# First stage of a hybrid decoder layer: the first two products' loads in written order, the later loads held back, a result tile moved to its own slots

## The chip, the cores and the metric

The kernel runs on one core of a Trainium2 chip. The metric is the device time of one execution in microseconds (us); the median of several runs counts. Engines are named as in the profile: PE does matmuls, PEld loads their weights, DVE, ACT and POOL do elementwise work, and SP issues nearly all DMAs from one in-order queue (SPq).

## What is computed

```
h = x @ w_in                  # x 1024 x 2048; w_in 2048 x 5392, float32
q_a, k_a, v_a, z_a, q_g, k_g, v_g, z_g, gk_lr = split(h)
y_a = sliding_window_attention(rope(q_a), rope(k_a), v_a, sinks) * silu(z_a)
y_g = rmsnorm(gated_linear_attention(q_g, k_g, v_g, decay(gk_lr))) * silu(z_g)
x = layer_norm(alpha * x + concat(y_a, y_g) @ w_out)
```

The first stage of the kernel, the only one that the change touches, computes `v_g = x @ w_v` with x 1024 x 2048 and w_v 2048 x 1024.

## The kernel before

The product for `v_g` is cut into 2 x 2 blocks and made by seven block products instead of eight (Strassen's scheme in Winograd's form). They run in the order 1, 2, 7, 5, 6, 4, 3 (`v_seq`). Each block product is 512 x 1024 by 1024 x 512 and has eight steps k = 0 to 7. A step takes one tile of x (128 x 512, 256 KB) and half of a weight tile (128 x 1024, 512 KB, two steps). Each float32 operand is split into a high part (a cast on ACT, L98) and a low part (a subtraction on DVE, L99), and a step is 4 row blocks times 3 matmuls: high by high (L696), high by low (L697), low by high (L698). So a step is 12 matmuls and a product 96.

Products 1 and 2 take x and w as they are in memory. Product 2 adds into product 1's banks, after `v_collect` has copied these out to the `u` tiles. Product 7 takes differences of two loaded tiles, made on POOL (L619 for x, L644 for w). Products 5, 6, 4 and 3 take running sums in tiles of their own, `xsum0` to `xsum7` and `wsum0` to `wsum3`: product 5 loads them first, and later products add or subtract one more loaded tile on POOL (L626 for x, L650 for w). Product 3's w is loaded as it is.

The pools set what can be loaded early: four slots for raw weights (tag `raw`), eight for split weights, 16 slots `xh` and 16 slots `xl` that loaded and split x tiles share. A load into a slot waits until the slot's last reader is done, and all that stands behind it in the SP queue waits with it.

Who stands where in an engine's queue is decided by the Tile scheduler, which goes by its own estimate of time and by `high_priority`. `fetch` (L600 to L605) issues every load of this stage at raised priority. `load_consts` (L122) loads the small tables and the tile `w_up`; it is called after product 1. `begin` (L551) loads `w_gk` for the second stage. `v_collect` for product 6 makes the result `o` (L668, L669) in a `raw` slot and writes it to memory from there (L670). `order(ins, head)` adds a scheduling dependency without a semaphore, so that the scheduler places `ins` behind `head`.

After this stage `begin(0)` loads x again for the second stage, with a few small matmuls (`lracc`, L283) between those of product 3.

Of the kernel before, what the change touches and what calls it, by code (L numbers as in the profile page):

```python
# [7 lines left out]
F32 = mybir.dt.float32  # L8
# [8 lines left out]
P = 128  # L17
# [55 lines left out]
def build(ctx: ExitStack, tc, xT, xr, w_e, w_v, w_gk, w_up, b_gk, cos_d, sin_d, cst_d, sinks, wn_d, w_out, g_d, b_d, out):  # L73
# [45 lines left out]
    one = cp.tile([P, 1], F32, name="one")  # L119
    mhalf = cp.tile([P, 2], F32, name="mhalf")  # L120

    def load_consts():  # L122
        wup = raw_p.tile([P, 2, 512], F32, name="raw", tag="raw")[:, 0]
        for t, src in ((cst, cst_d), (wup, w_up), (bgk, b_gk), (sink, sinks), (wn, wn_d)):
            SP.dma_start(t, src)
        V.tensor_scalar(nsink, sink, -1.0, None, ALU.mult)
        V.tensor_scalar(wnh, wn, 0.5, None, ALU.mult)
        A.copy(wuph, wup)
        V.tensor_tensor(wupl, wup, wuph.bitcast(F32), ALU.subtract)
        G.memset(neg, NEG)  # L130
        G.memset(one, 1.0)
        G.memset(mhalf, -0.5)
# [283 lines left out]
    def order(ins, head):  # L416
        with_dep = mybir.DependencyInfo(mybir.DependencyClass.NoSync, mybir.DependencyReason.DATA)
        tc.add_manual_dep(ins.ins, head.ins.name, with_dep, reason="after the bank's first")
        return ins
# [130 lines left out]
    def begin(H, i):  # L550

        c = ctxs[H]
        new_lr(H)
        parts[i], parts[i + 1] = [], []
        xr = []
        with tc.high_priority(2000):
            c["wgk"] = cp.tile([P, KT * 32], F32, name="wgk", tag="lr")
            SP.dma_start(c["wgk"], w_gk)
        for q in range(4):
            for j in range(2):  # L560
                xr += load(xT[H, q][:, 1024 * j:1024 * j + 1024])
                if j == 0 and q % 2 == 0:
                    wr = [load(jobs[i + n].src[0][:, 512 * q:512 * q + 1024]) for n in range(2)]
            for n in range(2):
                parts[i + n].append(split(wr[n][q % 2], w_p, "w"))
            for k in range(4 * q, 4 * q + 4):
                with tc.high_priority():
                    low_rank(c["lracc"], c["wgk"], k, xr[k])
                c["x"].append(split(xr[k], x_p, "x"))
        load_tabs(H)  # L570
# [26 lines left out]
    wsum = [vp.tile([P, 2, 512], F32, name=f"wsum{k}") for k in range(4)]  # L597
    us = {(i, t): vp.tile([P, 512], F32, name=f"u{i}{t}") for i in (1, 5, 7) for t in range(NB)}

    def fetch(t, src, pieces=1):  # L600
        with tc.high_priority(2000):
            for u in range(pieces):
                o = t[:, u:u + 1] if pieces > 1 else t
                SP.dma_start(o, src[:, 512 * u:512 * u + 512].unsqueeze(1) if pieces > 1 else src)
        return t  # L605

    def v_x(i, k):

        def block(h, g):
            return xT[h, 2 * g + k // 4][:, (k % 4) * T:(k % 4 + 1) * T]  # L610

        def raw(h, g, tag):
            return fetch(x_p.tile([P, T], F32, name="yr", tag=tag), block(h, g))

        if i in (1, 2, 4):
            a = raw(*{1: (0, 0), 2: (0, 1), 4: (1, 1)}[i], "xh")
        elif i == 7:
            a = raw(0, 0, "xh")
            G.tensor_tensor(a, a, raw(1, 0, "xl"), ALU.subtract)  # L619
        else:  # L620

            a = xsum[k]
            if i == 5:
                fetch(a, block(1, 0))
            b = raw(*{5: (1, 1), 6: (0, 0), 3: (0, 1)}[i], "xl")
            G.tensor_tensor(a, a, b, ALU.add if i == 3 else ALU.subtract)  # L626
        return split(a, x_p, "x")

    def v_w(i, kp):

        def block(g, F):
            return w_v[F, 2 * g + kp // 2][:, (kp % 2) * 1024:(kp % 2) * 1024 + 1024]

        def raw(g, F):
            r = raw_p.tile([P, 2, 512], F32, name="raw", tag="raw")
            if i == 1 and kp == 0:
                return fetch(r, block(g, F), 2)
            return fetch(r, block(g, F).rearrange("p (u c) -> p u c", u=2))

        if i in (1, 2, 3):  # L640
            r = raw(*{1: (0, 0), 2: (1, 0), 3: (1, 1)}[i])
        elif i == 7:
            r = raw(0, 1)
            G.tensor_tensor(r, r, raw(1, 1), ALU.add)  # L644
        else:

            r = wsum[kp]
            if i == 5:
                fetch(r, block(0, 0).rearrange("p (u c) -> p u c", u=2))
            G.tensor_tensor(r, r, raw(*{5: (0, 1), 6: (1, 1), 4: (1, 0)}[i]), ALU.add)  # L650
        return [split(r[:, u], w_p, "w") for u in range(2)]

    def v_collect(i, t, acc):
        u1, u5, u7 = (us[j, t] for j in (1, 5, 7))
        if i == 1:
            A.copy(u1, acc)
        elif i == 2:
            o = us[5, t]
            A.copy(o, acc)
            SP.dma_start(vd[0][0][:, t], o)  # L660
        elif i == 7:
            A.copy(u7, acc)
        elif i == 5:
            A.copy(u5, acc)
        elif i == 6:
            V.tensor_tensor(u1, u1, acc, ALU.add)
            V.tensor_tensor(u7, u7, u1, ALU.add)
            o = raw_p.tile([P, 512], F32, name="raw", tag="raw")  # L668
            V.tensor_tensor(o, u5, u7, ALU.subtract)  # L669
            SP.dma_start(vd[1][1][:, t], o)  # L670
            V.tensor_tensor(u5, u5, u1, ALU.subtract)
        else:
            o = u7 if i == 4 else u5
            V.tensor_tensor(o, o, acc, ALU.add)
            SP.dma_start(vd[1 if i == 4 else 0][0 if i == 4 else 1][:, t], o)

    v_seq = (1, 2, 7, 5, 6, 4, 3)
    v_xs, v_acc, v_n = {}, None, 0
    for vn, i in enumerate(v_seq):
        if i != 2:  # L680
            v_acc = []
            for t in range(NB):
                pool, tag = (mm, "mm") if v_n % 8 < 3 else (vo, "vo")
                v_acc.append(pool.tile([P, 512], F32, name="accv", tag=tag))
                v_n += 1
        for k in range(8):
            if (i, k) not in v_xs:
                v_xs[i, k] = v_x(i, k)
            if k % 2 == 0:
                wv = v_w(i, k // 2)  # L690
            if vn + 1 < len(v_seq):
                v_xs[v_seq[vn + 1], k] = v_x(v_seq[vn + 1], k)
            (xh, xl), (wh, wl) = v_xs[i, k], wv[k % 2]
            for t in range(NB):
                c = slice(t * P, t * P + P)
                PE.matmul(v_acc[t], xh[:, c], wh, start=(k == 0 and i != 2), stop=False, skip_group_check=True)  # L696
                PE.matmul(v_acc[t], xh[:, c], wl, start=False, stop=False, skip_group_check=True)  # L697
                PE.matmul(v_acc[t], xl[:, c], wh, start=False, stop=(k == 7 and i != 1), skip_group_check=True)  # L698
        for t in range(NB):
            v_collect(i, t, v_acc[t])  # L700
        if i == 1:
            load_consts()
    v_st.close()
    ap = side.enter_context(tc.tile_pool(name="ap", bufs=1, reuse_waits="tile"))
    gp = side.enter_context(tc.tile_pool(name="gp", bufs=1, reuse_waits="tile"))
# [11 lines left out]
    i = 0  # L717
# [248 lines left out]
```

## Time and profile before

| | |
|---|---|
| median of three runs | 1526.32 us (1522.78 to 1526.6) |
| the profiled execution's own time | 1524.23 us |
| its span | 1522.3 us |
| PE busy | 1416.3 us (93% of the span) |
| DVE / ACT / POOL busy | 941.6 / 624.6 / 384.3 us |
| mean granted TensorE clock | 0.971 of full speed |

A span is the time from the first to the last recorded instruction; 1.9 us of the execution lie outside of it. Busy shares are averages over stages with different limits, so the first stage has to be read from its own stretch, which is the first 253 us.

### The profile page before, as it was taken

To read this page: it belongs to the slowest core of one execution; us is meant where nothing else is said; L and a number is where in the kernel's file an instruction comes from. 1 tells how busy PE (TensorE), PEld (TensorE's weight loads), DVE (VectorE), ACT (ScalarE), POOL (GpSimd) and SP (SyncE) were. 2 spreads that over 40 slices of the span, in tenths; PEclk is the share of its full clock that TensorE was granted. 3 is DMA by queue.
4 is the path that set the end of the run, shared out by engine and by line. 5 is a ranking of instruction groups with operands and counts; after the bars stand their busy time and mean duration, and the time that the engine had idled before them with its cause. 6 is when DMAs were issued, how large, how long until landed. Compare 5 with 4: busy or idle time off the path is not lost.

```text
span 1522.3 us, 22157 instructions
## 1 busy us (share of the span) xinstructions
PE 1416.3 (93%) x8128; PEld 1133.0 (74%) x8128; DVE 941.6 (62%) x1545; ACT 624.6 (41%) x1335; POOL 384.3 (25%) x373
## 2 busy tenths in 40 slices
PE   3877679999999999999999999999999799999996
PEld 2664556888878877876888888887887588888885
DVE  3445476486666666568676657557658444455798
ACT  3322234454354354355454455344345324333320
POOL 0267041222323124122223222123221412023000
PEclk7899979999999999999999999999999899999998
DMA  9482167543443444445444443353345597766452
GB/s 333 152 268 93 35 224 239 166 148 122 153 141 122 136 144 133 135 152 170 156 157 149 142 144 120 121 163 113 116 160 159 154 344 242 241 187 217 138 213 111
DMA packets 116413, 251.66 MB, mean 165 GB/s; under 512 B 12368, under 2 KB 49232, under 8 KB 115152
## 3 DMA queue, kind: packets, MB, share of 16 engines
q1 hardware_dynamic: 115152, 248.15, 50.1%
q10 hardware_dynamic: 1152, 2.10, 0.4%
q8 instruction: 64, 1.05, 0.3%
q14 instruction: 45, 0.37, 0.1%
HBM read 205.63 MB, written 39.85 MB: 161 GB/s over the span
## 4 chain that ended last, share of the span: by engine, by line
PE 77%; DVE 6%; DMA 3%; ACT 2%; issue 2%; POOL 1%; SPq 0%; DVEq 0%; ACTq 0%; POOLq 0%
PE acc L159 15%; PE acc L161 14%; PE acc L160 14%; PE acco L798 6%; PE acco L796 6%; PE acco L797 6%; PE po L264 2%; PE accv L696 2%; PE accv L698 2%; PE accv L697 2%; DVE wl L99 1%; PE ps L232 1%; PE ps L233 1%; DMA yr<-yd 1%; DVE dd L316 1%
## 5 line engine op out<-in xcount | busy, mean ns | idle before, releaser
L99 DVE TENSOR_TENSOR wl<-raw,wh 128x512 fp32r<-128x512 f32 x408 | 317.8, 788 | 180.1 <-ACT wh L98 174.1
L159 PE MATMUL acc<-xh,wh 128*128 128x512 f32 x1088 | 428.7, 394 | 0.0
L160 PE MATMUL acc<-xl,wh 128*128 128x512 f32 x1088 | 428.0, 393 | 0.0
L161 PE MATMUL acc<-xh,wl 128*128 128x512 f32 x1088 | 427.3, 393 | 0.0
L98 ACT CAST wh<-raw 128x512 fp32r<-128x512 f32 x408 | 246.6, 618 | 270.3 <-PE acc L160 195.8
L161 PEld LDWEIGHTS acc<-xh,wl 128*128 128x128 f32 x1088 | 204.8, 188 | 47.3 <-issue 6.1
L159 PEld LDWEIGHTS acc<-xh,wh 128*128 128x128 f32 x1088 | 204.6, 188 | 45.5 <-issue 3.4
L160 PEld LDWEIGHTS acc<-xl,wh 128*128 128x128 f32 x1088 | 204.6, 188 | 41.9 <-issue 1.8
L797 PE MATMUL acco<-wl,xh 128*128 128x512 f32 x416 | 162.8, 391 | 0.0
L796 PE MATMUL acco<-wh,xh 128*128 128x512 f32 x416 | 162.5, 392 | 0.0
L798 PE MATMUL acco<-wh,xl 128*128 128x512 f32 x416 | 162.4, 391 | 0.0
L696 PE MATMUL accv<-wh,xh 128*128 128x512 f32 x224 | 94.6, 430 | 70.3 <-ACT xh L98 46.2
L99 DVE TENSOR_TENSOR xl<-yr,xh 128x512 fp32r<-128x512 f32 x88 | 68.4, 781 | 132.9 <-ACT xh L98 131.9
L98 ACT CAST xh<-yr 128x512 fp32r<-128x512 f32 x88 | 54.0, 620 | 212.5 <-POOL yr L775 71.5
L696 PEld LDWEIGHTS accv<-wh,xh 128*128 128x128 f32 x224 | 45.3, 203 | 89.0 <-ACT xh L98 54.3
L697 PE MATMUL accv<-wl,xh 128*128 128x512 f32 x224 | 94.2, 421 | 0.5 <-DVE wl L99 0.4
L797 PEld LDWEIGHTS acco<-wl,xh 128*128 128x128 f32 x416 | 78.7, 189 | 17.0 <-DVE wl L99 0.5
L796 PEld LDWEIGHTS acco<-wh,xh 128*128 128x128 f32 x416 | 78.7, 189 | 16.3
L798 PEld LDWEIGHTS acco<-wh,xl 128*128 128x128 f32 x416 | 78.5, 189 | 16.4
L580 POOL TENSOR_TENSOR raw<-raw 128x256 f32<-128x256 f32 x32 | 26.1, 814 | 224.5 <-DMA raw<-in_w_out_dram 163.5
L698 PE MATMUL accv<-wh,xl 128*128 128x512 f32 x224 | 80.2, 416 | 1.6 <-DVE xl L99 1.5
L775 POOL TENSOR_TENSOR yr<-yr 128x512 f32<-128x512 f32 x32 | 44.2, 1383 | 145.7 <-DMA yr<-yd 107.7
(186 smaller groups left out, 1918.5 us busy)
## 6 DMA issues: line engine op xcount, KB each, us to landing
raw<-in_w_e_dram SPq DMA_DIRECT2D x136, 512.0 KB, 4.3
yr<-yd SPq DMA_DIRECT2D x88, 256.0 KB, 4.6
yr<-in_xT_dram SPq DMA_DIRECT2D x64, 256.0 KB, 5.3
raw<-in_w_out_dram SPq DMA_DIRECT2D x128, 128.0 KB, 2.7
td<-raw SPq DMA_DIRECT2D x32, 512.0 KB, 3.4
raw<-td SPq DMA_DIRECT2D x32, 512.0 KB, 5.3
raw<-in_w_v_dram SPq DMA_DIRECT2D x31, 512.0 KB, 5.1
raw<-in_w_out_dram SPq DMA_DIRECT2D x24, 512.0 KB, 3.9
```

The source lines that it names most:

```text
L98: A.copy(hi, src)
L99: V.tensor_tensor(lo, src, hi.bitcast(F32), ALU.subtract)
L159: PE.matmul(acc, wh[:, c], xh, start=(k == 0), stop=False)
L160: PE.matmul(acc, wh[:, c], xl, start=False, stop=False)
L161: PE.matmul(acc, wl[:, c], xh, start=False, stop=(k == KT - 1))
L696: PE.matmul(v_acc[t], xh[:, c], wh, start=(k == 0 and i != 2), stop=False, skip_group_check=True)
L697: PE.matmul(v_acc[t], xh[:, c], wl, start=False, stop=False, skip_group_check=True)
L698: PE.matmul(v_acc[t], xl[:, c], wh, start=False, stop=(k == 7 and i != 1), skip_group_check=True)
L775: G.tensor_tensor(a, a, b, ALU.add if sign > 0 else ALU.subtract)
L796: PE.matmul(acc, yh[:, c], wh, start=(first and k == 0), stop=False, skip_group_check=True)
L797: PE.matmul(acc, yh[:, c], wl, start=False, stop=False, skip_group_check=True)
L798: PE.matmul(acc, yl[:, c], wh, start=False, stop=(last and k == 7), skip_group_check=True)
```

## The change

- The loads of products 1 and 2 are issued at ordinary priority and kept in the order of the program. Product 2's x tiles are written two at a time into product 1's steps 4 to 7, instead of one per step.
- The first loads of the running sums are placed behind named matmuls: `xsum`k behind the last matmul of product 2's step k, `wsum`kp behind that of product 7's step 2 kp.
- The constants and `w_gk` are placed behind product 6's last matmul, and `load_consts` is called after product 6.
- Product 6's result `o` gets two slots of its own instead of `raw` slots.

```diff
-    def load_consts():
+    def load_consts(head):
         wup = raw_p.tile([P, 2, 512], F32, name="raw", tag="raw")[:, 0]
         for t, src in ((cst, cst_d), (wup, w_up), (bgk, b_gk), (sink, sinks), (wn, wn_d)):
-            SP.dma_start(t, src)
+            order(SP.dma_start(t, src), head)
...
             c["wgk"] = cp.tile([P, KT * 32], F32, name="wgk", tag="lr")
-            SP.dma_start(c["wgk"], w_gk)
+            ins = SP.dma_start(c["wgk"], w_gk)
+            if H == 0:
+                order(ins, v_last[6, 7])
...
-    def fetch(t, src, pieces=1):
-        with tc.high_priority(2000):
+    v_last = {}
+
+    def fetch(t, src, pieces=1, head=None):
+        with tc.high_priority(2000 if head or len(v_last) > 8 else 0):
             for u in range(pieces):
                 o = t[:, u:u + 1] if pieces > 1 else t
-                SP.dma_start(o, src[:, 512 * u:512 * u + 512].unsqueeze(1) if pieces > 1 else src)
+                ins = SP.dma_start(o, src[:, 512 * u:512 * u + 512].unsqueeze(1) if pieces > 1 else src)
+                if head:
+                    order(ins, head)
+                elif len(v_last) <= 8:
+                    tc.keep_in_program_order(ins)
         return t
...
             if i == 5:
-                fetch(a, block(1, 0))
+                fetch(a, block(1, 0), head=v_last[2, k])
...
             if i == 5:
-                fetch(r, block(0, 0).rearrange("p (u c) -> p u c", u=2))
+                fetch(r, block(0, 0).rearrange("p (u c) -> p u c", u=2), head=v_last[7, 2 * kp])
...
-            o = raw_p.tile([P, 512], F32, name="raw", tag="raw")
+            o = vp.tile([P, 512], F32, name="o", tag="o", bufs=2)
             V.tensor_tensor(o, u5, u7, ALU.subtract)
...
             if vn + 1 < len(v_seq):
-                v_xs[v_seq[vn + 1], k] = v_x(v_seq[vn + 1], k)
+                for k2 in ((k,) if vn else (2 * k - 8, 2 * k - 7)):
+                    if k2 >= 0:
+                        v_xs[v_seq[vn + 1], k2] = v_x(v_seq[vn + 1], k2)
...
-                PE.matmul(v_acc[t], xl[:, c], wh, start=False, stop=(k == 7 and i != 1), skip_group_check=True)
+                v_last[i, k] = PE.matmul(v_acc[t], xl[:, c], wh, start=False, stop=(k == 7 and i != 1), skip_group_check=True)
         for t in range(NB):
             v_collect(i, t, v_acc[t])
-        if i == 1:
-            load_consts()
+        if i == 6:
+            load_consts(v_last[6, 7])
```

Three places of the built queues are shown. In all of them `yr` is a loaded x tile, `raw` a loaded weight tile, and the number behind a name tells tiles apart.

The SP queue, start of the program, before: behind the first loads of product 1 stand all eight `xsum` loads (and then the four of `wsum`).

```order
L604 DMA raw_212<-in_w_v_dram 128x1024
L604 DMA yr_164<-in_xT_dram 128x512
L604 DMA raw_270<-in_w_v_dram 128x1024
L604 DMA raw_328<-in_w_v_dram 128x1024
L604 DMA xsum0_119<-in_xT_dram 128x512
L604 DMA xsum1_120<-in_xT_dram 128x512
L604 DMA xsum2_121<-in_xT_dram 128x512
L604 DMA xsum3_122<-in_xT_dram 128x512
L604 DMA xsum4_123<-in_xT_dram 128x512
L604 DMA yr_182<-in_xT_dram 128x512
L604 DMA xsum5_124<-in_xT_dram 128x512
```

The same place with the change; `yr_147`, `yr_176`, `yr_194`, `yr_222`, `yr_240`, `yr_280`, `yr_310` and `yr_350` are product 1's x tiles, the other `yr` up to `yr_362` product 2's.

```order
L608 DMA yr_176<-in_xT_dram 128x512
L608 DMA yr_194<-in_xT_dram 128x512
L608 DMA raw_200<-in_w_v_dram 128x1024
L608 DMA yr_222<-in_xT_dram 128x512
L608 DMA yr_240<-in_xT_dram 128x512
L608 DMA raw_246<-in_w_v_dram 128x1024
L608 DMA yr_256<-in_xT_dram 128x512
L608 DMA yr_262<-in_xT_dram 128x512
L608 DMA yr_280<-in_xT_dram 128x512
L608 DMA yr_286<-in_xT_dram 128x512
L608 DMA yr_292<-in_xT_dram 128x512
L608 DMA yr_310<-in_xT_dram 128x512
```

The sums' loads have left the head of the queue (the first, `xsum0`, stands at place 27 now), and the x tiles of product 2 stand between those of product 1.

The SP queue where product 2's result is written out (`vd0_0` from `u50` and so on), before; `yr_511` and `yr_513` are the pair of product 7's step 4.

```order
L604 DMA raw_888<-in_w_v_dram 128x1024
L604 DMA yr_511<-in_xT_dram 128x512
L604 DMA yr_513<-in_xT_dram 128x512
L604 DMA raw_938<-in_w_v_dram 128x1024
L604 DMA raw_988<-in_w_v_dram 128x1024
L660 DMA vd0_0_101<-u50_135 128x512
L660 DMA vd0_0_101<-u51_136 128x512
```

The same with the change; `yr_467` and `yr_469` are the pair of product 7's step 3.

```order
L608 DMA wsum0_127<-in_w_v_dram 128x1024
L668 DMA vd0_0_101<-u50_135 128x512
L608 DMA raw_825<-in_w_v_dram 128x1024
L668 DMA vd0_0_101<-u51_136 128x512
L668 DMA vd0_0_101<-u52_137 128x512
L608 DMA raw_875<-in_w_v_dram 128x1024
L608 DMA yr_467<-in_xT_dram 128x512
L668 DMA vd0_0_101<-u53_138 128x512
L608 DMA yr_469<-in_xT_dram 128x512
```

Before, five of product 7's eight pairs stand ahead of the write; now three do, and the fourth stands behind it.

The SP queue at the end of product 6, before; `raw_1261` to `raw_1408` are product 4's weights, `vd1_1` the write of product 6's result.

```order
L670 DMA vd1_1_104<-raw_1235 128x512
L670 DMA vd1_1_104<-raw_1241 128x512
L604 DMA yr_1197<-in_xT_dram 128x512
L670 DMA vd1_1_104<-raw_1247 128x512
L604 DMA raw_1261<-in_w_v_dram 128x1024
L604 DMA raw_1310<-in_w_v_dram 128x1024
```

With the change:

```order
L125 DMA cst_72<-in_cst_dram 128x705
L125 DMA raw_1244<-in_w_up_dram 128x512
L608 DMA raw_1261<-in_w_v_dram 128x1024
L608 DMA raw_1310<-in_w_v_dram 128x1024
L608 DMA yr_1090<-in_xT_dram 128x512
L608 DMA raw_1359<-in_w_v_dram 128x1024
L125 DMA bgk_75<-in_b_gk_dram 128x4
L125 DMA sink_76<-in_sinks_dram 128x16
L125 DMA wn_77<-in_wn_dram 128x2
L678 DMA vd1_1_104<-o_1222 128x512
L608 DMA yr_1108<-in_xT_dram 128x512
L608 DMA raw_1408<-in_w_v_dram 128x1024
L608 DMA raw_1469<-in_w_v_dram 128x1024
```

Three of product 4's four weight loads have moved ahead of the write of the result. On DVE, with the change, these rows end with the first low part of product 4's weights (`wl_1265`):

```order
L675 TENSOR_TENSOR u70_139<-u70_139,u10_131 128x512
L675 TENSOR_TENSOR u71_140<-u71_140,u11_132 128x512
L99 TENSOR_TENSOR xl_1064<-yr_1061,xh_1063 128x512
L675 TENSOR_TENSOR u72_141<-u72_141,u12_133 128x512
L675 TENSOR_TENSOR u73_142<-u73_142,u13_134 128x512
L677 TENSOR_TENSOR o_1222<-u50_135,u70_139 128x512
L129 TENSOR_TENSOR wupl_74<-raw_1244,wuph_73 128x512
L677 TENSOR_TENSOR o_1228<-u51_136,u71_140 128x512
L679 TENSOR_TENSOR u50_135<-u50_135,u10_131 128x512
L99 TENSOR_TENSOR xl_1093<-yr_1090,xh_1092 128x512
L679 TENSOR_TENSOR u51_136<-u51_136,u11_132 128x512
L99 TENSOR_TENSOR wl_1265<-wsum0_127,wh_1264 128x512
```

That subtraction has stayed behind most of product 6's collecting work (the four rows of L674 stand ahead of this piece).

## Rows read from the trace of the kernel before

**Rows 1.** Windows by product, core 0: stretch, length, busy and count by engine, clock, DMA.

```profile
6.00:63.00 57.00, 31.78 (x94) 23.63 (x95) 22.12 (x33) 17.45 (x30) 4.70 (x2) 0.76 0.76 264
63.00:85.50 22.50, 22.50 (x99) 18.32 (x99) 9.22 (x9) 8.13 (x15) 10.79 (x6) 1.00 0.57 167
85.50:120.30 34.80, 24.65 (x96) 18.63 (x96) 15.08 (x17) 9.50 (x19) 24.57 (x12) 0.90 0.83 274
120.30:157.20 36.90, 26.92 (x99) 18.15 (x97) 17.93 (x16) 11.60 (x22) 24.77 (x16) 0.95 0.25 84
157.20:181.20 24.00, 21.50 (x95) 17.75 (x95) 6.20 (x10) 9.40 (x19) 0.00 (x0) 1.00 0.07 23
181.20:200.00 18.80, 0.74 (x4) 0.28 (x3) 13.44 (x23) 1.37 (x3) 3.12 (x2) 0.62 0.51 170
200.00:226.60 26.60, 26.10 (x101) 20.54 (x102) 20.96 (x22) 11.39 (x20) 14.62 (x8) 0.88 0.62 205
226.60:253.40 26.80, 26.80 (x113) 17.51 (x112) 16.85 (x25) 11.56 (x21) 5.86 (x5) 1.00 0.63 205
```

**Rows 2.** Who waited for whom, first 270 us: total, times, longest.

```profile
PE accv L696 <- ACT xh L98: 46.2, 15, 13.9
PE accv L696 <- ACT wh L98: 24.1, 2, 18.1
```

**Rows 3.** Timeline of the SP queue: start, length, line, transfer, count.

```profile
4.04 4.52 SPq L604 DMA_DIRECT2D xsum<-in_xT_dram  x5
...
29.25 3.83 SPq L604 DMA_DIRECT2D yr<-in_xT_dram  x7
...
187.94 0.93 SPq L670 DMA_DIRECT2D vd<-raw  x2
...
190.39 1.11 SPq L604 DMA_DIRECT2D raw<-in_w_v_dram  x2
```

**Rows 4.** Timeline of PE: start, length, line, operation, idle time before and its releaser.

```profile
6.01 2.07 PE L696 MATMUL accv<-wh,xh 128*128 128x512 f32 x4 [6.01 <-ACT wh L98]
...
59.08 0.50 PE L696 MATMUL accv<-wh,xh 128*128 128x512 f32 x1 [3.59 <-ACT xh L98]
...
106.91 0.80 PE L696 MATMUL accv<-wh,xh 128*128 128x512 f32 x1 [5.50 <-ACT xh L98]
112.96 0.49 PE L696 MATMUL accv<-wh,xh 128*128 128x512 f32 x1 [1.30 <-ACT xh L98]
117.82 0.50 PE L696 MATMUL accv<-wh,xh 128*128 128x512 f32 x1 [1.83 <-ACT xh L98]
...
202.14 0.80 PE L697 MATMUL accv<-wl,xh 128*128 128x512 f32 x1
```

**Rows 5.** Windows of two short stretches, columns as in Rows 1.

```profile
0.00:10.00 10.00, 3.99 (x9) 3.14 (x10) 3.19 (x5) 4.79 (x7) 1.72 (x10) 1.00 0.75 234
16.50:22.00 5.50, 5.43 (x12) 3.81 (x12) 0.69 (x1) 0.02 (x1) 0.00 (x0) 0.51 1.03 402
```

**Rows 6.** DMA issues of the page: transfer, count, size, median us to landing.

```profile
yr<-in_xT_dram SPq DMA_DIRECT2D x64, 256.0 KB, 5.3
```

**Rows 7.** Groups by line and shape, first 270 us: count, busy us, mean ns.

```profile
L650 POOL TENSOR_TENSOR wsum<-wsum,raw 128x1024 f32<-128x1024 f32 x12 | 30.6, 2568 | 54.0 <-DMA raw<-in_w_v_dram 45.4 <-issue 4.4 <-DVE wl L99 3.4
...
L619 POOL TENSOR_TENSOR yr<-yr 128x512 f32<-128x512 f32 x8 | 11.2, 1395 | 11.9 <-DMA yr<-in_xT_dram 11.9
```

**Rows 8.** Timeline of ACT where product 1's results are copied out.

```profile
63.02 1.56 ACT L656 COPY u<-accv 128x512 f32<-128x512 f32 x3 [3.41 <-PE accv L698]
```

**Rows 9.** Timeline of DVE behind product 6.

```profile
181.22 2.48 DVE L666 TENSOR_TENSOR u<-u,accv 128x512 f32<-128x512 f32 x4 [15.92 <-PE accv L698]
...
190.24 0.68 DVE L671 TENSOR_TENSOR u<-u,u 128x512 f32<-128x512 f32 x1
...
199.90 4.97 DVE L99 TENSOR_TENSOR wl<-wsum,wh 128x512 fp32r<-128x512 f32 x2 [5.34 <-ACT wh L98]
```

**Rows 10.** Timeline of POOL in the same place.

```profile
196.88 10.24 POOL L650 TENSOR_TENSOR wsum<-wsum,raw 128x1024 f32<-128x1024 f32 x4 [40.46 <-DMA raw<-in_w_v_dram]
```

## The prediction

> **What bounds the kernel now.** I read the stage product by product, in windows whose edges are the ends of the products [rows 1]. From a window I take three things: its length, the time in which PE did nothing, and the granted clock. The measure is the stretch 63.00 to 85.50 (product 2): 99 matmuls in 22.50 us at clock 1.00, so 2.73 us for a step of 12 and 21.8 us for a product of 96. Seven products would be 153 us; the stage takes 253.4 less the 6.0 of its start. The loss lies in four windows. Product 1 takes 57.0 us instead of 21.8, product 7 34.8, product 5 36.9, and between 181.2 and 200.0 PE does nearly nothing (0.74 us busy).
>
> Next the waits: PE's first matmul of a step waits for a cast on ACT, 46.2 us for x and 24.1 us for weights [rows 2]. What the casts wait for shows in the queue that feeds them [rows 3]. From 4.04 on SP issues `xsum` tiles, which product 5 uses at 120; most of product 1's x tiles go out only at 29.25. The second hole shows in the same rows: product 6's results leave at 187.94, and only at 190.39 does SP issue product 4's first weights, since both use `raw` slots. The first matmul of product 4 that needs a low part of weights runs at 202.14 [rows 4].
>
> **The change part by part.** I follow the queues of the changed build and price every step with rows of the profile before; all times are on that profile's clock.
>
> *Products 1 and 2.* The first three loads stay what they are, so the first matmul stays at 6.0 [rows 4]. For step 0 I take the price of a slow step, 5.5 us at clock 0.51 [rows 5], and for seven more 2.73: 6.0 + 5.5 + 19.1 = 30.6. Does the data keep up? In its first 10 us the kernel moves 2.34 MB, and later 402 GB/s [rows 5]; in the new order 2.36 MB reach to step 4's x tile, which PE wants at about 20 us. So transfers are not the limit. Two of product 1's tiles wait for slots: step 6's x behind the eighth matmul of step 1 (about 13), and step 7's behind the tenth of step 3 (about 19). With 5.3 us to land [rows 6] both are there 3 us or more before PE wants them.
>
> Then a new wait begins. On ACT product 2's first weight cast stands behind the four copies of product 1's result and the cast of product 2's last x tile. ACT does these 0.52 us apart (three in 1.56) [rows 8]: six of them and a start are 3.4 us, in which PE stands. After a stop of 3.59 us now [rows 4] comes slow work; I charge one slow step, 2.8 us more. Product 2 ends at 30.6 + 3.4 + 2.8 + 21.8 = 58.6 instead of 85.5: **-26.9 us**. Both ends: -30 without the slow work, -7.5 if all of product 1 ran at 5.5 us a step.
>
> *Product 7.* Its lead is gone. Now five of its eight pairs of x tiles are loaded ahead of the write of product 2's results; with the change three are, and the write, with two weight loads, holds the SP queue until product 2 ends. The fourth pair then goes out after two copies, two casts and a subtraction (2.8 us) and its second half 0.8 us later, lands after 5.3, is subtracted on POOL in 1.4 [rows 7] and cast in 0.6: 10.9 us after product 2's end, where PE wants it after three steps, 8.2. That is a stall of 2.7. Behind it POOL takes sums for products 5 and 6 (2.57 each [rows 7]) between the x differences, and some of these wait for weights that PE has just released. The nearest rows are the three steps that run in this way now: PE waited 5.50, 1.30 and 1.83 us [rows 4], 2.9 a step. Five steps, 3 to 7, give 14.4 us. Now the window loses 10.15 us to idling and 2.85 to the clock (34.8 - 24.65, and the rest above 21.8) [rows 1]; I keep the latter. So 21.8 + 14.4 + 2.9 = 39.1 instead of 34.8: **+4.3 us**. Bounds: -10.8, if it ran like product 6 (24.0), and +22.9 (below).
>
> *Products 5 and 6.* ACT, DVE and POOL have the same order here as before, with the same waits for slots: **0**. The table loads that now come here find the DMA engines 25% and 7% busy [rows 1]; without this cover they would cost the 2.2 us that their 0.9 MB (705 and twice 512 columns by 128 rows by 4 bytes) take at 402 GB/s.
>
> *Product 4.* Three of its four weight loads now run during products 5 and 6, and POOL, idle throughout product 6 [rows 1], adds them up. What is late next is DVE: the first low part of weights stands behind 15 other operations after product 6's end. Now the same number, from 181.22, has run when the operation at 190.24 starts [rows 9], so this low part is done at 190.24 + 0.68 = 190.9, where it took until 202.14 [rows 4]: **-11.2 us**. Bounds: 0, if something else holds PE as long, and -18.8, the whole window.
>
> *Product 3.* It gives some back. The load for its step 2 now stands in the SP queue behind the four writes of product 4's result, which wait for four additions (2.48 us [rows 9]): issued 3.5 us after product 4's end, landed after 5.3, added and cast 2.0 later, so at 10.8, where PE wants it after two steps and a group of `lracc`, at about 6.5: 4.3 us. The x tiles for the `lracc` groups behind step 3 wait for a split whose slot step 2 frees: 0.6 + 0.7 + 5.3 = 6.6 us, of which step 3 hides 2.7: 3.9 us. **+8.2 us**; the window has no idling now (26.80 of 26.80 [rows 1]), so below lies 0, and above 12, a third such wait.
>
> The last part, the tile `o` in its own slots, frees `raw` slots and adds no instruction; its effect is in product 4's sum. All later stages keep their orders but for single rows, so they move as a whole.
>
> Sum: -26.9 + 4.3 + 0 - 11.2 + 8.2 = -25.6 us. Against the profiled execution's own 1524.2 this gives 1498.6; the median lies 2.1 us higher, within the runs' spread of 3.8. I say **1498 us**.
>
> **The port that POOL and DVE share.** A low split takes 0.68 us on a free DVE; while POOL made four weight sums in a row (196.88 to 207.1 [rows 10]), two splits took 4.97 us [rows 9], 2.5 each. So as a mechanism of this kernel: if every low split of product 7's five late steps met a POOL sum, PE would wait 1.8 us more in each, 9.0 in all, and the time would be 1507.6. The Trainium skill, SBUF — State Buffer, Who interferes with whom, says that a DVE instruction with two SBUF inputs and a GpSimd instruction that reads SBUF exclude each other, and that the second to issue "fully blocks". By that rule, the trace agrees: 2.5 us is about one sum of 2.57. It speaks against a change that puts POOL's sums into the stretch where DVE splits weights; for it only part of the splits meet a sum, since POOL itself waits for loads in that stretch.
>
> **Rivals.**
> - *Product 7 flows.* Its weights and first differences are ready before product 2 ends, and if the late pairs were too it would take 24.0 like product 6: 1483.5. Against it stands the write in the SP queue.
> - *The port*, 1507.6, as above.
> - *The slots do nothing.* Something else holds product 4 for the same time, and product 3 stays as it is: -26.9 + 4.3, 1501.6.
> - *Slow clock.* Product 1's window has 0.76 now [rows 1]; if its seven further steps stayed at 5.5 us: 19.4 more, 1518. Against it: the stretch from 63.00 ran at 1.00 throughout.
> - *Product 7 starves: the other side.* If each late step waited for a whole chain of load, weight sum, x difference and cast (5.3 + 2.6 + 1.4 + 0.6 = 9.9 us), the five would make product 7 57.7 us long, +22.9 and 1517 in all. From 11.3 us a step on the kernel is not faster, and from 12.2 clearly slower (1529). For it: several of these loads wait for POOL's sums. Against it: now the worst such step waited 5.50, not 8.6.
>
> That the change doesn't do what it says is excluded by the order of the built queues: the sums' loads and tables stand where the diff puts them, though without a semaphore.
>
> **How the numbers follow.** Chances: the forecast 0.53 (its own range 1489 to 1505), product 7 flows 0.12, the port 0.12, the slots do nothing 0.08, slow clock 0.06, the starving at 9.9 us 0.05, from 11.3 on 0.04. The range 1483 to 1512 holds the first four, less what lies beyond its edges. A difference under 0.3% (4.6 us) can't be told from none here. Faster by more have all cases but the last, less a little for two of them together: 0.94; within 0.02; slower 0.04.
>
> **What would show it.** In the profile after: product 2 ends near 58.6, with one stop of about 3.4 us between products 1 and 2 that a cast ends; product 7 is longer than 34.8 us, with waits for casts of x from step 3 on, behind POOL; products 5 and 6 together stay within 2 us of 60.9; the hole before product 4 shrinks to about 10 us and ends on DVE instead of ACT; product 3 shows two stops of about 4 us. It is wrong if product 1 still waits for x tiles, if product 7's steps are above 9 us, or if the second stage starts with stops that it does not have now.

## The result, and the profile after

The changed kernel takes 1502.64 us (median of three runs, 1501.11 to 1504.4) against 1526.32 us: a ratio of 0.9852, with an interval of 0.9824 to 0.988. That is 23.7 us by the medians and 22.9 by the spans of the profiled executions (1522.3 and 1499.4). The forecast was 1498.

Windows of the changed kernel's profile, one for each product in the order 1, 2, 7, 5, 6, 4, 3, with the columns and the kind of edges of [rows 1] (the hole before product 4 is counted in product 4's window here):

```profile
5.60:28.99 23.39, 23.39 (x96) 18.93 (x96) 14.02 (x22) 12.70 (x23) 0.00 (x0) 1.00 0.82 286
28.99:55.00 26.01, 23.52 (x97) 19.27 (x97) 10.82 (x16) 11.36 (x22) 10.25 (x5) 0.93 0.96 323
55.00:97.24 42.24, 29.12 (x97) 21.22 (x95) 22.31 (x17) 11.20 (x20) 29.98 (x15) 0.84 0.85 293
97.24:133.65 36.41, 26.47 (x96) 18.02 (x96) 18.33 (x17) 11.12 (x21) 25.66 (x17) 0.95 0.42 148
133.65:162.50 28.85, 23.84 (x98) 19.23 (x98) 10.92 (x11) 10.63 (x20) 6.52 (x3) 0.94 0.00 1
162.50:194.60 32.10, 23.89 (x98) 19.27 (x97) 26.14 (x42) 9.51 (x17) 5.94 (x2) 0.84 0.60 196
194.60:229.75 35.15, 27.89 (x116) 18.75 (x115) 15.44 (x25) 11.74 (x21) 9.73 (x8) 1.00 0.53 165
```

Product by product against [rows 1]:

| | before | after | difference | forecast |
|---|---|---|---|---|
| end of product 2 | 85.5 | 55.0 | -30.5 | -26.9 |
| product 7 | 34.8 | 42.2 | +7.4 | +4.3 |
| products 5 and 6 | 60.9 | 65.3 | +4.4 | 0 |
| hole and product 4 | 45.4 | 32.1 | -13.3 | -11.2 |
| product 3 | 26.8 | 35.2 | +8.3 | +8.2 |
| end of the stage | 253.4 | 229.75 | -23.7 | -25.6 |

The signs came out as forecast except for products 5 and 6, which were to cost nothing. After the stage 0.8 us of the gain is lost.

PE's stops in the changed kernel (timeline of PE, columns as in [rows 4]; lines stand 8 to 10 further down than before, so that L706 to L708 are the three matmuls that were L696 to L698):

```profile
31.50 1.38 PE L706 MATMUL accv<-wh,xh 128*128 128x512 f32 x4 [2.49 <-ACT wh L98]
...
68.51 0.80 PE L706 MATMUL accv<-wh,xh 128*128 128x512 f32 x1 [5.19 <-ACT xh L98]
...
75.88 0.50 PE L706 MATMUL accv<-wh,xh 128*128 128x512 f32 x1 [2.12 <-ACT xh L98]
...
140.77 1.40 PE L708 MATMUL accv<-wh,xl 128*128 128x512 f32 x4 [2.52 <-DVE xl L99]
...
171.75 0.79 PE L707 MATMUL accv<-wl,xh 128*128 128x512 f32 x1 [8.21 <-DVE wl L99]
...
200.79 0.50 PE L706 MATMUL accv<-wh,xh 128*128 128x512 f32 x1 [2.34 <-ACT xh L98]
...
207.23 0.50 PE L706 MATMUL accv<-wh,xh 128*128 128x512 f32 x1 [1.67 <-ACT xh L98]
```

One stop stands between products 1 and 2. Product 7 has its first three steps without any, then the longest (5.19), 2.12 and three more that are not shown (2.29, 1.57 and 1.82). Product 6 starts with a stop of 2.49 us that a cast ends (not shown; it was 2.50 before) and then has a new one of 2.52, which ends on DVE. The hole before product 4 is 8.21 us and ends on a low part of weights.

What DVE and POOL did around the new stop in product 6 and the hole (DVE first, then POOL):

```profile
135.12 2.83 DVE L99 TENSOR_TENSOR wl<-wsum,wh 128x512 fp32r<-128x512 f32 x1 [3.73 <-ACT wh L98]
137.88 7.06 DVE L99 TENSOR_TENSOR xl<-xsum,xh 128x512 fp32r<-128x512 f32 x8
...
161.99 2.48 DVE L674 TENSOR_TENSOR u<-u,accv 128x512 f32<-128x512 f32 x4 [16.45 <-PE accv L708]
...
171.00 0.69 DVE L99 TENSOR_TENSOR wl<-wsum,wh 128x512 fp32r<-128x512 f32 x1
```

```profile
132.72 7.45 POOL L658 TENSOR_TENSOR wsum<-wsum,raw 128x1024 f32<-128x1024 f32 x3
```

These three sums are product 4's. Before, its four sums began at 196.88 [rows 10], behind product 6; now three of them stand at the start of product 6, beside the splits that product 6 waits for: one split takes 2.83 us, and the next eight 7.06.

### The profile page after: what moved, and what is told of

Read it like the earlier page. It is cut to its first block, busy times and chain, and to the rows that moved or that the text cites. A ratio compares the mean times of both kernels' runs of the same rounds, so it can differ in the third digit from the quotient of the medians.

```text
span 1499.4 us, 22160 instructions
## 1 busy us (share of the span) xinstructions
PE 1413.4 (94%) x8128; PEld 1133.0 (76%) x8128; DVE 941.5 (63%) x1545; ACT 625.2 (42%) x1335; POOL 381.9 (25%) x373
## 4 chain that ended last, share of the span: by engine, by line
PE 72%; DVE 4%; DMA 3%; ACT 1%; issue 1%; POOL 1%; SPq 1%; DVEq 0%; ACTq 0%; POOLq 0%
PE acc L159 15%; PE acc L160 14%; PE acc L161 14%; PE acco L806 6%; PE acco L808 6%; PE acco L807 6%; PE po L264 2%; DMA yr<-yd 1%; PE ps L232 1%; PE ps L233 1%; DMA rs<-rq 1%; PE pt L254 1%; PE pa L333 1%; DVE wl L99 1%; POOL yr L785 1%
## 5 line engine op out<-in xcount | busy, mean ns | idle before, releaser
L99 DVE TENSOR_TENSOR wl<-raw,wh 128x512 fp32r<-128x512 f32 x408 | 314.0, 782 | 190.0 <-ACT wh L98 185.6
L98 ACT CAST xh<-yr 128x512 fp32r<-128x512 f32 x88 | 54.1, 621 | 172.9 <-POOL yr L785 62.8
L706 PE MATMUL accv<-wh,xh 128*128 128x512 f32 x224 | 89.5, 422 | 38.6 <-ACT xh L98 30.6
L706 PEld LDWEIGHTS accv<-wh,xh 128*128 128x128 f32 x224 | 44.4, 199 | 58.2 <-ACT xh L98 39.9
L181 POOL TENSOR_TENSOR rs<-rs,sin 128x512 f32<-128x512 f32 x18 | 31.1, 1729 | 198.0 <-DMA rs<-rq 198.0
L708 PE MATMUL accv<-wh,xl 128*128 128x512 f32 x224 | 74.5, 416 | 2.8 <-DVE xl L99 2.5
```

Source lines behind the costliest of these rows:

```text
L98: A.copy(hi, src)
L99: V.tensor_tensor(lo, src, hi.bitcast(F32), ALU.subtract)
L708: v_last[i, k] = PE.matmul(v_acc[t], xl[:, c], wh, start=False, stop=(k == 7 and i != 1), skip_group_check=True)
```

## Experiments

All times are medians; ratios are to the kernel before, run on the same chip. The lengths come from one profiled execution each. Here a product ends where ACT or DVE begins to read its first result (product 7 of the changed kernel: from 53.16 to 96.57, 43.4), so they stand up to 2 us beside the windows above. They are to be compared within this table. The kernel before took 1525.4 to 1528.2 us in the rounds of the experiments, so times of different rounds are compared by their ratios. e4_thin_sums and e9_pairs_thin leave out most of POOL's weight sums.

| kernel | us | ratio, interval | 1 ends | 2 | 7 | 5 | 6 | 4 | 3 |
|---|---|---|---|---|---|---|---|---|---|
| before | 1526.3 | | 63.0 | 23.1 | 34.1 | 36.5 | 24.6 | 44.0 | 27.5 |
| changed | 1502.6 | 0.9852, 0.9824 to 0.988 | 28.4 | 24.8 | 43.4 | 36.4 | 29.0 | 33.2 | 34.0 |
| e5_no_heads | 1516.9 | 0.9932, 0.9902 to 0.9962 | 42.7 | 25.0 | 44.8 | 35.3 | 27.4 | 33.5 | 33.3 |
| e6_heads_only | 1517.4 | 0.9941, 0.9924 to 0.9959 | 52.5 | 23.2 | 39.8 | 33.5 | 27.4 | 32.8 | 33.5 |
| e1_o_raw (lengths: e1b_o_raw) | 1508.6 | 0.986, 0.9832 to 0.9889 | 29.6 | 23.2 | 47.2 | 36.4 | 26.2 | 46.9 | 26.2 |
| e2_o_only | 1529.3 | 1.0002, 0.9984 to 1.0019 | 62.8 | 24.5 | 36.5 | 40.9 | 37.3 | 22.5 | 31.9 |
| e12_tables_back | 1512.4 | 0.9913, 0.9887 to 0.9938 | 31.1 | 27.6 | 45.9 | 40.6 | 36.4 | 23.7 | 30.5 |
| e3_write_act | 1504.0 | 0.9832, 0.9806 to 0.9858 | 28.3 | 24.8 | 43.9 | 36.4 | 29.0 | 33.1 | 33.7 |
| e4_thin_sums | 1498.4 | 0.9791, 0.9757 to 0.9826 | 28.6 | 24.8 | 41.0 | 37.4 | 26.2 | 31.7 | 34.0 |
| e7_pairs_first | 1498.6 | 0.9812, 0.9775 to 0.9849 | 28.7 | 24.8 | 28.8 | 48.5 | 29.0 | 33.2 | 32.0 |
| e8_sums_later | 1502.1 | 0.9836, 0.9807 to 0.9865 | 30.1 | 27.2 | 23.0 | 44.1 | 37.1 | 33.1 | 35.2 |
| e9_pairs_thin | 1487.1 | 0.9742, 0.9703 to 0.9781 | 29.1 | 23.2 | 29.8 | 38.8 | 24.6 | 31.8 | 37.9 |
| e10_late_collect | 1487.1 | 0.9739, 0.971 to 0.9768 | 30.2 | 23.2 | 43.9 | 36.5 | 26.2 | 23.3 | 28.8 |

### The first two products: two halves

e5_no_heads takes the heads of the sums' loads away, e6_heads_only the written order.

```diff
-                fetch(a, block(1, 0), head=v_last[2, k])
+                fetch(a, block(1, 0))
...
-                fetch(r, block(0, 0).rearrange("p (u c) -> p u c", u=2), head=v_last[7, 2 * kp])
+                fetch(r, block(0, 0).rearrange("p (u c) -> p u c", u=2))
```

> The changed kernel without the two head arguments: the first loads of the sums are not held behind named matmuls, all else as changed. Theory that the sums' loads at the head of the queue are what starved product 1: they come back to the front, product 1 takes 50 us or more again instead of 23.4, product 7 gets its lead back and loses 7 us less: 1515 to 1525 us. Rival, the written order of the first loads does it: loads kept in order stay ahead of the sums', product 1 stays at 23 to 26 us, and the time at 1500 to 1505.

```diff
-        with tc.high_priority(2000 if head or len(v_last) > 8 else 0):
+        with tc.high_priority(2000):
...
-                elif len(v_last) <= 8:
-                    tc.keep_in_program_order(ins)
```

> The changed kernel with all loads at raised priority again and none kept in written order; the sums' loads stay behind their matmuls. Theory that the sums' loads are the whole cause: product 1 stays near 23 to 28 us and the time within 4 us of 1503. Rival, the order among the first two products' own loads matters as well: in this queue four weight loads stand ahead of product 1's third x tile and wait for `raw` slots; product 1 takes 35 us or more, 1512 us or more in all.

The SP queue of e5_no_heads at the start (timeline as in [rows 3]):

```profile
0.73 4.16 SPq L608 DMA_DIRECT2D xsum<-in_xT_dram  x8
4.93 3.58 SPq L608 DMA_DIRECT2D wsum<-in_w_v_dram  x4
9.71 0.33 SPq L608 DMA_DIRECT2D yr<-in_xT_dram  x1
```

All twelve loads of the sums stand ahead of the first x tile, and PE begins at 18.84 instead of 5.59; behind that product 1 runs without a stop. In e6_heads_only PE begins at 5.93, but product 1 has five stops of 1.2 to 3.8 us. e6_heads_only came out as its rival had it. e5_no_heads lies in the time range of its theory, but product 1 ends at 42.7 instead of 50 or more, late by its start, and product 7 gets no lead back (44.8). With only one of the halves the whole change is worth 9 to 10 us instead of 23, and only both together let product 1 start early and run through.

### The slots and the tables

e1_o_raw undoes the slots of `o` alone; e2_o_only makes that edit alone in the kernel before.

```diff
-            o = vp.tile([P, 512], F32, name="o", tag="o", bufs=2)
+            o = raw_p.tile([P, 512], F32, name="raw", tag="raw")
```

> The changed kernel with the tile `o` back in a `raw` slot, all else as changed. Slots theory: only the two slots of their own let product 4's weights be loaded and added up before product 6 ends. Then the stretch from product 6's end to product 4's end goes back from 32.1 to about 45.4 us, product 6 falls from 28.9 to about 24.0, because POOL's three sums no longer run at its start, and product 3 gets back up to 8.3 us: 1503 to 1511 us. Rival, the moved tables: it was not the slots but the moved loads of the tables that cleared the place; then product 6 and product 4 stay at 28.9 and 32.1 us and the time at 1502.6.

> The kernel of the run e1_o_raw once more, for its profile (that of the first lay in a disturbed run). The time of the first, 1508.6, stands between the two theories' times. Slots theory: product 6 near 24 us and the stretch behind it to product 4's end 40 us or more, against 28.9 and 32.1 with the slots. Rival: both as with the slots, and the 6 us lie in product 3 or later.

> The kernel before with nothing changed but the tile `o` in two slots of its own. Slots theory: the stretch behind product 6 falls from 45.4 to about 32 us, product 6 rises from 24.0 to about 29 if POOL's sums collide with its first splits, and product 3 rises by 0 to 8.3: 1513 to 1523 us. If product 3's loss belongs to the slots it rises to 35 us here as well; if it belongs to the other parts it stays at 26.8. Rival, the slots do nothing without the moved tables: 1526.

e12_tables_back undoes the move of the tables and of `w_gk`.

```diff
-            if H == 0:
-                order(ins, v_last[6, 7])
...
-        if i == 6:
-            load_consts(v_last[6, 7])
+        if i == 1:
+            load_consts(v_last[1, 7])
```

> The changed kernel with the tables and `w_gk` back at their old place behind product 1; the slots of `o` and the rest stay. In this queue product 4's four weight loads and product 3's four stand between the x loads of products 7, 5 and 6, as in e2_o_only, and wait there for POOL's sums; with the tables moved they stand behind product 5's and 6's loads. Theory that the tables' move is what keeps product 4's loads out of the way, so that the slots pay only together with it: product 5 rises from 36.4 to about 40 us, product 6 from 28.9 to 35 or more, product 4 falls from 32.1 to about 22.5: 1506 to 1518 us. Rival, as the prediction had it, the tables cost and bring nothing: every product as in the changed kernel and 1501 to 1505 us.

Without the slots the hole is back: product 4 takes 46.9 us, product 6 falls to 26.2 and product 3 to 26.2, so the slots bring 13.7 us and cost 2.8 and 7.8 elsewhere. (The lengths are those of e1b_o_raw, the same kernel in a single execution of 1514.05 us, 5.5 above the median of e1_o_raw; 3.8 us of that are in product 7, which the edit doesn't explain.) e1_o_raw's 1508.6 lies 4.6 us above e3_write_act on the same chip, whose product lengths are the changed kernel's. In e2_o_only the slots alone change nothing (1.0002): the hole goes entirely (product 4 takes 22.5 us), but products 5, 6 and 3 lose 21.5 us. e12_tables_back shows the same, as its theory had it: product 4 takes 23.7 us, products 5 and 6 lose 11.6 against the changed kernel. Its SP queue during product 5:

```profile
120.88 0.33 SPq L606 DMA_DIRECT2D raw<-in_w_v_dram  x1
121.26 0.90 SPq L606 DMA_DIRECT2D yr<-in_xT_dram  x2
130.11 0.33 SPq L606 DMA_DIRECT2D raw<-in_w_v_dram  x1
130.54 0.85 SPq L606 DMA_DIRECT2D yr<-in_xT_dram  x2
```

A weight load of a later product, which waits for one of the four `raw` slots, stands ahead of every two x tiles; from 110.85 to 150.96 the queue lets two of these go every 9 to 11 us, where PE needs 5.5 for two steps. In the changed kernel the seventeen x loads from 81.84 on go out without a weight load between them. So the tables, priced at nothing, decide where product 4's loads stand.

### What holds product 7

e3_write_act moves product 2's result writes to ACT's queue. e4_thin_sums makes POOL's weight sums short: it adds 16 of 512 columns and leaves out the rest.

```diff
-            SP.dma_start(vd[0][0][:, t], o)
+            A.dma_start(vd[0][0][:, t], o)
```

> The changed kernel with product 2's four result writes issued from ACT's queue, so that they no longer stand in SP's. Queue theory: product 7's fourth pair goes out about 3 us earlier, the stop of 5.19 us at step 3 falls to about 2.5 and some slow work behind it goes: product 7 falls from 42.2 to 37 to 39 us, 1498 to 1500 us in all. Rival, POOL paces product 7: the x difference stands behind POOL's weight sums and every later step waits for both; the stop moves but the product stays within 1.5 us of 42.2, and the time at 1501 to 1503.

```diff
-            G.tensor_tensor(r, r, raw(*{5: (0, 1), 6: (1, 1), 4: (1, 0)}[i]), ALU.add)
+            b = raw(*{5: (0, 1), 6: (1, 1), 4: (1, 0)}[i])
+            G.tensor_tensor(r[:, :, :16], r[:, :, :16], b[:, :, :16], ALU.add)
```

> The changed kernel with POOL's twelve weight sums for products 5, 6 and 4 cut to 16 of 512 columns: it leaves out the rest of these sums, while all loads, casts and splits stay. Theory of POOL and its port: product 7's late stops shrink (POOL is free for the x differences, and low splits are back at 0.7 us), product 7 falls from 42.2 to 30 to 34 us, product 6 from 28.9 to 24: about 1486 to 1490 us. Queue theory: in product 7 the loads come late whatever POOL does, so it stays at 39 to 42 us; only product 6 gets its 4.9 us back: about 1496 to 1498 us.

Neither moves product 7 much: 43.9 and 41.0 against 43.4. So e3_write_act refutes its queue theory, which took the write for the gate; e4_thin_sums came out as its queue theory had it, but for product 6, which gets back 2.8 us and not 4.9. The SP queue of the changed kernel, and below it that of e3_write_act, where the fourth x pair goes out:

```profile
57.40 0.33 SPq L608 DMA_DIRECT2D raw<-in_w_v_dram  x1
57.78 0.45 SPq L608 DMA_DIRECT2D yr<-in_xT_dram  x1
58.73 0.33 SPq L668 DMA_DIRECT2D vd<-u  x1
59.17 0.37 SPq L608 DMA_DIRECT2D yr<-in_xT_dram  x1
```

```profile
52.07 5.91 SPq L608 DMA_DIRECT2D raw<-in_w_v_dram  x2
58.02 1.50 SPq L608 DMA_DIRECT2D yr<-in_xT_dram  x2
```

With the write gone the pair still goes out at 58.02: it stands behind two weight loads, and the second goes out only at 57.64, over 5 us behind the first, when a `raw` slot comes free (DVE's last read of it ends at 57.61). e7_pairs_first therefore keeps e3's edit and places the second loads of products 5's and 6's weight sums behind product 7's last x pair.

```diff
-            G.tensor_tensor(a, a, raw(1, 0, "xl"), ALU.subtract)
+            b = raw(1, 0, "xl")
+            v_pair[k] = issued[-1]
+            G.tensor_tensor(a, a, b, ALU.subtract)
...
-            return fetch(r, block(g, F).rearrange("p (u c) -> p u c", u=2))
+            return fetch(r, block(g, F).rearrange("p (u c) -> p u c", u=2), head=head)
...
-            G.tensor_tensor(r, r, raw(*{5: (0, 1), 6: (1, 1), 4: (1, 0)}[i]), ALU.add)
+            G.tensor_tensor(r, r, raw(*{5: (0, 1), 6: (1, 1), 4: (1, 0)}[i], v_pair[7] if i != 4 else None), ALU.add)
```

> The changed kernel with product 7's x pairs issued ahead of the second loads of products 5's and 6's weight sums, and product 2's results written from ACT's queue as in e3_write_act. Theory that the x pairs stand behind weight loads for later products, which wait for one of four `raw` slots, and their differences behind these sums on POOL: product 7 falls from 42.2 to 24 to 30 us, with no stop over 2 us, and the time to 1489 to 1496 us if product 5's weights come in time. Rival, the port or the clock paces product 7: it stays at 39 us or more and the time at 1499 or more.

Product 7 falls to 28.8 us as the queue theory said, but product 5 takes 12 us more and the time misses its range (1498.6 us, 1489 to 1496 expected): the wait has moved. DVE and POOL of e7_pairs_first at that place:

```profile
81.82 18.72 DVE L99 TENSOR_TENSOR wl<-wsum,wh 128x512 fp32r<-128x512 f32 x8
```

```profile
78.76 10.66 POOL L661 TENSOR_TENSOR wsum<-wsum,raw 128x1024 f32<-128x1024 f32 x4
89.38 1.71 POOL L637 TENSOR_TENSOR xsum<-xsum,yr 128x512 f32<-128x512 f32 x1
91.06 5.58 POOL L661 TENSOR_TENSOR wsum<-wsum,raw 128x1024 f32<-128x1024 f32 x2
97.33 2.66 POOL L661 TENSOR_TENSOR wsum<-wsum,raw 128x1024 f32<-128x1024 f32 x1 [0.68 <-DVE wl L99]
```

Eight low splits take 2.34 us each while POOL works through its sums. e8_sums_later changes POOL's order on top of this, e9_pairs_thin makes its weight sums short (e4's edit on e7).

```diff
-                fetch(a, block(1, 0), head=v_last[2, k])
+                fetch(a, block(1, 0), head=v_pair[7])
...
+            v_pair[i, k] = issued[-1]
...
-v_pair[7] if i != 4 else None), ALU.add)
+{5: v_pair[7], 6: v_pair.get((5, 7))}.get(i)), ALU.add)
```

> The kernel of e7_pairs_first with two more places: the first x loads of the sums stand behind product 7's last x pair, and the second loads of product 6's weight sums behind product 5's last x load, so that POOL has product 5's sums ahead of product 6's. Theory that product 5's loss in e7_pairs_first (48.5 against 36.4 us) comes from POOL's order: product 6's four sums stand ahead of product 5's second x sum: product 5 falls to 30 to 37 us with product 7 at 24 to 28, and the time to 1482 to 1489 us. Rival, POOL and DVE together have no more room, whatever the order: products 7 and 5 stay at 74 to 78 us together and the time at 1496 to 1500.

> The kernel of e7_pairs_first with POOL's weight sums for products 5, 6 and 4 cut to 16 of 512 columns; it leaves out the rest of these sums. If POOL's sums and the slow low splits beside them make product 5's loss, product 5 falls from 48.5 to 26 to 34 us, product 7 stays at 24 to 28 and product 6 at about 25, in all 1474 to 1484 us. If the loads make it, product 5 stays above 42 us and the time above 1490.

Neither branch of e8_sums_later came (1502.1 us), and the order only moves the loss on: products 7, 5 and 6 together take 108.8 us in the changed kernel, 106.2 in e7_pairs_first and 104.3 in e8_sums_later. The short sums alone give 104.6, both together 93.1. So two limits lie side by side: the loads' order in the SP queue, and POOL's sums with the splits beside them. Taking one away shows the other. They are not all of it: with both away product 5 still takes 38.8 us, between the two branches of e9_pairs_thin (26 to 34, above 42).

### The stop in product 6 and the hole

e10_late_collect holds product 4's weight loads behind its fifth x tile, and product 6's collecting behind product 4's first two low parts.

```diff
+            if i == 4:
+                v_ld[k] = issued[-1]
...
+raw(*{5: (0, 1), 6: (1, 1), 4: (1, 0)}[i], v_ld[4] if i == 4 else None), ALU.add)
...
-            V.tensor_tensor(u1, u1, acc, ALU.add)
+            order(V.tensor_tensor(u1, u1, acc, ALU.add), wls[0])
...
+                if (i, k) == (4, 0):
+                    wls.append(low[-1])
+                    for t in range(NB):
+                        v_collect(6, t, v_old[t])
```

> The changed kernel with two edits at product 6 and none ahead of it. Product 4's weight loads stand behind its fifth x tile in the SP queue, which waits for product 6's first step, so that POOL's three sums run after DVE's splits of product 6; and the collecting of product 6 stands on DVE behind the first two low parts of product 4's weights, with the writes of the result behind the loads. Theory of the port: the stop of 2.5 us in product 6's first step and the slow work behind it go, 28.9 to 24 to 25 us. Theory that DVE's order alone makes the hole of 8.2 us: it falls to 1 to 3 us, product 4 takes 22 to 26 us with it instead of 32.1. Product 3 gets back some of its loss, since its loads no longer stand behind the writes: 27 to 35 us. In all 1480 to 1491. Rivals: the stop in product 6 stays at 2.5 us because a cast or a load makes it (no gain there); the hole stays above 6 us since the weights' sums are late now.

Windows of e10_late_collect for products 6, 4 and 3, by the edges of the table:

```profile
133.79:159.94 26.15, 23.66 (x97) 19.11 (x96) 14.39 (x19) 15.12 (x28) 10.37 (x4) 0.93 0.62 181
159.94:183.25 23.31, 23.31 (x104) 19.30 (x103) 21.47 (x34) 7.48 (x13) 8.71 (x3) 1.00 0.42 146
183.25:212.08 28.83, 26.14 (x110) 17.41 (x109) 13.38 (x22) 8.84 (x17) 7.20 (x6) 1.00 0.50 162
```

Its DVE and POOL at the start of product 6 (the splits are L101 here):

```profile
135.90 0.69 DVE L101 TENSOR_TENSOR wl<-wsum,wh 128x512 fp32r<-128x512 f32 x1 [3.73 <-ACT wh L100]
136.91 4.91 DVE L101 TENSOR_TENSOR xl<-xsum,xh 128x512 fp32r<-128x512 f32 x8 [0.31 <-ACT xh L100]
```

```profile
145.95 10.37 POOL L663 TENSOR_TENSOR wsum<-wsum,raw 128x1024 f32<-128x1024 f32 x4 [12.42 <-DMA raw<-in_w_v_dram]
```

With POOL's sums 13 us later the eight splits take 4.91 us instead of 7.06, the one before them 0.69 instead of 2.83, and the stop of 2.52 is gone: product 6 is 2.8 us shorter, not the 4 to 5 that were expected, since PE still runs below its full clock there (0.93). The hole is gone altogether, and product 3 gets 5.1 us back. At 1487.1 us this is the fastest kernel of the study among those that leave nothing out, and faster than the changed one: the interval of its ratio (0.971 to 0.9768) lies wholly below the changed kernel's (0.9824 to 0.988).

## Why the prediction was right, and where its steps were off

**Products 1 and 2 (-26.9, measured -30.5).** The mechanism holds, and every charge was a little high: the first matmul 0.4 us earlier, product 1 at clock 1.00 and 1.2 shorter than charged, the stop 2.49 instead of 3.4, and 1.7 us of slow work behind it (23.52 busy against 21.8) instead of 2.8. The stop ends on the cast that the prediction named.

**Product 7 (+4.3, measured +7.4).** The size that was off is the clock. PE idles 13.1 us in the window, where the prediction had 14.4, but works 29.12 us at clock 0.84: 7.3 above the free 21.8, where the prediction kept the 2.9 of before. The step that failed is a cause: "the write, with two weight loads, holds the SP queue until product 2 ends". Without the write the pair goes out at the same time; one of the weight loads alone holds it, by its `raw` slot (e3_write_act, e7_pairs_first). The first stop, priced at 2.7 us, is 5.19: the pair's second half goes out 4.2 us after product 2's end, where 3.6 were charged, and lands 7.2 us later (POOL starts on it at 66.55), where 5.3 were charged. The DMA engines are busy throughout this stretch (a window of the changed kernel, columns as in [rows 1]):

```profile
53.16:68.50 15.34, 10.17 (x45) 8.07 (x43) 9.84 (x8) 6.71 (x12) 8.85 (x6) 0.94 1.01 373
```

The prediction asked only for product 1 whether the transfers keep up. No run separates their share of this stop from that of the queue's order.

The rival of the port was to cost 9.0 us here: short sums give back 2.4, and that includes POOL's own time.

**Products 5 and 6 (0, measured +4.4).** This step failed. The prediction used the idle POOL of product 6 as cover for product 4's sums, and did not ask which splits DVE has there. The sums fall on product 6's first splits; moving them (e10_late_collect) or making them short (e4_thin_sums) brings 2.8 us back. The rest of the loss is slow clock behind the product's first stop (0.93 to 0.94, against 1.00 in [rows 1]). It is there without the sums too: e1b_o_raw, e4_thin_sums and e10_late_collect all take 26.2 us; e9_pairs_thin takes 24.6, as before. Why it comes now is open. Pricing the tables at nothing was wrong in another way: product 5, in which they go out now, is no longer than before (36.4 against 36.9 us), but without their move the slots' gain is lost in products 5 and 6 (e2_o_only, e12_tables_back).

The Trainium skill, SBUF — State Buffer, Who interferes with whom, calls the port that DVE and GpSimd share an exclusive lock. The traces agree in kind: beside POOL, DVE gets about one split done for each POOL instruction (2.34 us each in e7_pairs_first, where a weight sum takes 2.67, against 0.61 in e10_late_collect without POOL beside it), and in a later stretch of e10_late_collect POOL waits beside DVE (last section).

**The hole and product 4 (-11.2, measured -13.3).** The hole ends on DVE as forecast, and the first low part is done 9.2 us after product 6's end (171.69 from 162.50) where the forecast had 9.7. e10_late_collect shows that DVE's order makes this hole: two low parts stand ahead of the collecting there, product 4's first weight loads and sums come later than in the changed kernel, and the hole is gone. Of the other 2.1 us 0.5 lie here and 1.6 in product 4's remaining steps. What the account of the loads lacks is the tables: the slots alone let the loads come early, but so early that products 5 and 6 lose what product 4 gains; that they come behind product 5's x loads takes the tables' place as well.

**Product 3 (+8.2, measured +8.3).** The size was right, the shape less: not two stops of about 4 us but six of 0.3 to 2.3, together 7.3, and 1.1 us more work on PE (27.89 against 26.80). The longest, 2.34 at step 1, was not in the prediction, so that the size fits is in part luck. The load for step 2 (at 199.07) does go out behind product 4's four writes:

```profile
195.85 2.48 SPq L683 DMA_DIRECT2D vd<-u  x4
198.43 0.59 SPq L91 DMA_DIRECT2D raw<-in_xT_dram  x1
199.07 1.55 SPq L608 DMA_DIRECT2D yr<-in_xT_dram  x3
```

PE gets this tile at 207.23. That the loss belongs to the slots, and with them to what stands in the SP queue, shows where they are undone: 26.2 us in e1b_o_raw.

So the forecast held because errors of opposite sign nearly met: products 1, 2 and 4 gained 5.7 us more than priced, and products 7, 5 and 6 lost 7.5 more; product 3 and the later stages add 0.9. That is 2.7 us of span; the median lies 1.5 us above the profiled execution's 1501.11, and the forecast had rounded its sum down by 0.6. That these errors nearly met is luck.

Open: how much of the limit in products 7 to 6 is POOL's own time and how much the slow splits, since short sums remove both; why product 6 lost its full clock; and what holds product 5 in e9_pairs_thin.

## What to carry to other kernels

A load that is moved ahead also moves the work that it releases: ask which engine takes it up there, and which instructions of its neighbour then run beside it. Idle time on POOL is no free cover while DVE has splits that PE waits for.

In an in-order queue a transfer waits for the latest of all the gates ahead of it. To take one gate away may show nothing (e3_write_act); list the waits of everything that stands ahead, and move the transfer rather than the gate.

Price each stop of PE with the slow matmuls that follow, and give that price a range: in product 7 13.1 us of stops came with 7.3 us of slow work, while the same stop ahead of product 6 cost 0 or about 2 us of it.

## What the runs showed of the hardware that was not expected

Which of DVE and POOL slows down beside the other is not fixed. In e7_pairs_first a low split grows from 0.61 to 2.34 us, nearly four times, while a weight sum on POOL takes 2.67 us on average, against 2.4 where it runs fastest. In e10_late_collect, behind product 6, it is POOL that waits: one of its x sums, which take 1.3 us elsewhere, takes 6.02, while DVE starts an operation every 0.60 us.

```profile
174.29 6.02 POOL L639 TENSOR_TENSOR xsum<-xsum,yr 128x512 f32<-128x512 f32 x1 [9.52 <-DMA yr<-in_xT_dram]
```

PE's full clock does not hang on the length of a stop alone. Ahead of product 6 PE stops for 2.49 or 2.50 us in the kernel before and in e1b_o_raw, e4_thin_sums, e9_pairs_thin and e10_late_collect, and nothing else stops it in the product. Yet the granted clock of the product was 1.00 before and in e9_pairs_thin, and 0.93 in the other three.
